# Feed-forward gate and up by seven block products, and two weight sums of every pair by adding transfers

## The chip, the cores and the metric

One core of a Trainium2 chip runs the whole program. The metric is device time in microseconds (us). The engines are TensorE (PE, matmuls), VectorE (DVE), ScalarE (ACT), GpSimd (POOL) and SyncE (SP, which issues the transfers). TensorE reads its operands from the on-chip memory SBUF and adds into the banks of PSUM.

## The reference

512 tokens (16 more, "meta", stand ahead of them) of width 1024 pass three blocks: a block of attention, a linear recurrence and a gated feed-forward part, and then two layers of a short convolution and retention. What matters here:

```python
u = rms_norm(h, norm_ffn_w[l])                      # feed-forward part; D_FF = 2816 = 22 tiles of 128
h = h + (silu(u @ w_ffn_gate[l]) * (u @ w_ffn_up[l])) @ w_ffn_down[l]
...
xn = _rmsnorm(h, pre_norm_g[l])                     # each of the two layers
proj = xn @ w_in[l] + b_in[l]
c_h, c_b, c_c, c_z, r_q, r_k, r_v, r_z, g_a, g_b = split(proj)
y_a = short_conv(c_h, c_b, c_c, c_z) @ w_out
y_b = retention(r_q, r_k, r_v, r_z) @ w_out
y = (sigmoid(g_a) * y_a + sigmoid(g_b) * y_b) @ w_o[l]
```

Everything is float32.

## The kernel before

Activations lie transposed: 128 features on the partitions, eight tiles for the width of 1024, tokens along the free axis (528, or 512 without meta). A weight tile is 128 x 1024: one output tile of 128 features, all 1024 inputs.

**Three matmuls per product.** Each float32 operand is split into a rounded high part (ACT's copy to float32r) and the rest as a low part (DVE's subtraction). `mm3` (L148 to L150) forms high x high, low x high, high x low. `unit` loads a weight tile by SP into a raw buffer `wraw` and splits it (L126 ACT, L127 DVE) into `whi` and `wlo`. There are three buffers of each of these tags.

**Seven products.** In the layers, two output tiles are formed together (`seven`): a 2 x 2 block scheme that needs seven block products where eight would do. The blocks are two output tiles, two halves of the 1024 inputs and two halves of the tokens. `pair` loads both weight tiles `sa` (a11, a12) and `sb` (a21, a22) and forms four sums of weight blocks on DVE (L201, L202, L203, L205), 128 x 512 each, which are split as well (L188 ACT, L189 DVE). The operands on the token side (n5, n6, m7, and m4 in place of a block of xs) are formed once by the generator `operands` in `layer2`, beside two plain tiles. Each product is 12 matmuls (L223); a pair is 84, of 264 columns in layer 0 and 258 in layer 1. `keep` copies a partial result out of PSUM, `sink` turns the products into outputs. `a22` and `s4` of a pair are used late, in the next pair's turn.

**Feed-forward part** (`ffn`, L869). For each of 22 tiles a gate and an up product by `mm3`: the first two tiles in two halves of the tokens (the second half waits for its normalization), the others at 512 columns. SiLU is ACT's; `fg = fg * ps` (L884) and the split into `act` are DVE's and ACT's. Then eight rows of the down projection sum over all 22 tiles, the last three rows in two halves.

**What sets the order.** Each engine runs its instructions in the order in which a scheduler laid them down when the program was built, by priority and data flow; `high_priority` moves a weight's load, splits and sums ahead. SP issues transfers in order, and each waits for its buffer to be free.

Of the kernel before, what the change touches and what calls it, by code (L numbers as in the profile page):

```python
# [59 lines left out]
class Builder:  # L60
# [52 lines left out]

    def unit(self, src, pool=None):

        nc = self.nc
        cols = src.shape[-1]
        raw = self.wp.tile([P, 1040], F32, name="wraw", tag="wraw", bufs=3)[:, :cols]
        hi, lo = (
            (pool or self.wp).tile([P, 1024 if pool else 1040], F32R, name=f"w{n}", tag=f"w{n}", bufs=KEEP if pool else 3)[:, :cols]  # L120
            for n in ("hi", "lo")
        )

        with self.tc.high_priority(offset=AHEAD):
            nc.sync.dma_start(raw, src)
            nc.scalar.activation(hi, raw, AF.Copy)  # L126
            nc.vector.tensor_tensor(lo, raw, hi.bitcast(F32), ALU.subtract)  # L127
        return hi, lo

    def loadr(self, dst, src):  # L130

        n = int(np.prod(dst.shape[1:]))
        t = self.wp.tile([P, 1040], F32, name="wraw", tag="wraw", bufs=3)[:, :n]
# [43 lines left out]
    def pair(self, sa, sb, pool):  # L177
# [6 lines left out]
        def split(names, src, where):  # L184
            n = src.shape[-1]
            hi, lo = ((self.wp if where == "w" else pool).tile(
                [P, 1040 if where == "w" else 1024], F32R, name=f"{where}{x}", tag=f"{where}{x}", bufs=3)[:, :n] for x in ("hi", "lo"))
# [5 lines left out]
        with self.tc.high_priority(offset=PAIRAHEAD):  # L193
            ra, rb = (self.wp.tile([P, 1040], F32, name="wraw", tag="wraw", bufs=3)[:, :1024] for _ in range(2))
            nc.sync.dma_start(ra, sa)
            nc.sync.dma_start(rb, sb)
            split(("a11", "a12"), ra, "w")
            s23, s14 = (pool.tile([P, 1056], F32, name="ws", tag="ws", bufs=2) for _ in range(2))
            s1, s2, s3, s4 = s14[:, :H], s23[:, :H], s23[:, H : 2 * H], s14[:, H : 2 * H]
            a11, a12, a21, a22 = ra[:, :H], ra[:, H:], rb[:, :H], rb[:, H:]  # L200
            nc.vector.tensor_tensor(s1, a21, a22, ALU.add)  # L201
            nc.vector.tensor_tensor(s2, s1, a11, ALU.add)  # L202
            nc.vector.tensor_tensor(s3, a21, a11, ALU.add)  # L203
            split(("s2", "s3"), s23[:, : 2 * H], "s")
            nc.vector.tensor_tensor(s4, s2, a12, ALU.add)  # L205
            split(("s1", "s4"), s14[:, : 2 * H], "s")
            split(("a22",), a22, "w")
        return parts

    def seven(self, units, X, n, pool):  # L210
# [29 lines left out]
        for sa, sb, sink in units:  # L240
# [628 lines left out]
    def ffn(self, h, acc, xs, last_chain):  # L869
        tc, nc, d = self.tc, self.nc, self.d  # L870
        NF = 22
        SPLIT = 3
        with tc.tile_pool(name="ff", bufs=1) as ff:
            act = tuple(ff.tile([P, NF, NX], F32R, name=f"act{s}") for s in "hl")
            gs = {}

            def gate(i, a, n, up):
                if i not in gs:
                    gs[i] = ff.tile([P, NX], F32, name="fg", tag="fg", bufs=3)
                c = slice(a - NM, a - NM + n)  # L880
                g = gs[i][:, c]
                for ps, _, _ in self.fproj(d["w_up" if up else "w_gate"][i], xs, ((a, n),)):
                    if up:
                        nc.vector.tensor_tensor(g, g, ps, ALU.mult)  # L884
                        self.split(act[0][:, i, c], act[1][:, i, c], g)
                    else:
                        nc.scalar.activation(g, ps, AF.Silu)
# [16 lines left out]
            for i, segs in parts:  # L904
                us = []
                for a, k in ((0, 8), (8, 8), (16, 6)):
                    hi, lo = self.unit(d["w_down"][i, :, a * P : (a + k) * P])
                    us.append((hi, lo, range(a, a + k), 0))
# [635 lines left out]
```

## Time and profile before

| | us |
|---|---|
| median of 3 runs | 2385.03 (2383.64 to 2392.14) |
| the profiled execution | 2390.16 |
| its span, first to last instruction | 2388.4 |
| mean granted clock of TensorE | 0.993 of full speed |
| TensorE busy | 2338.1 (98%) |
| VectorE busy | 1453.8 (61%) |
| ScalarE busy | 999.6 (42%) |
| POOL busy | 374.8 (16%) |

Busy times come from one profiled execution. A matmul's duration overlaps the next one's; the pace is read from the starts. POOL issues no transfer in this kernel.

### The profile page before, as it was taken

To read this page: it belongs to the slowest core of one execution; us is meant where nothing else is said; L and a number is where in the kernel's file an instruction comes from. 1 tells how busy PE (TensorE), PEld (TensorE's weight loads), DVE (VectorE), ACT (ScalarE), POOL (GpSimd) and SP (SyncE) were. 2 spreads that over 40 slices of the span, in tenths; PEclk is the share of its full clock that TensorE was granted. 3 is DMA by queue.
4 is the path that set the end of the run, shared out by engine and by line. 5 is a ranking of instruction groups with operands and counts; after the bars stand their busy time and mean duration, and the time that the engine had idled before them with its cause. 6 is when DMAs were issued, how large, how long until landed. Compare 5 with 4: busy or idle time off the path is not lost.

```text
span 2388.4 us, 40000 instructions
## 1 busy us (share of the span) xinstructions
PE 2338.1 (98%) x16322; PEld 2177.8 (91%) x16322; DVE 1453.8 (61%) x2560; ACT 999.6 (42%) x1751; POOL 374.8 (16%) x431
## 2 busy tenths in 40 slices
PE   8999989999999999999999999999999999999997
PEld 7888879888889999999999999999898888999987
DVE  5377786333336755555478996566455555899853
ACT  6244474222225443333335564444332423455633
POOL 3043442000003221111000020042111101000200
PEclk9999999999999999999999999999999999999999
DMA  4211203232335322222122232413222222232222
GB/s 155 87 44 59 72 19 106 97 97 90 90 100 186 119 89 84 72 83 80 63 89 98 98 105 99 131 69 111 89 84 87 77 80 78 90 107 101 97 95 71
DMA packets 67625, 217.97 MB, mean 91 GB/s; under 512 B 8816, under 2 KB 14576, under 8 KB 67440
## 3 DMA queue, kind: packets, MB, share of 16 engines
q1 hardware_dynamic: 67440, 215.40, 27.4%
q8 instruction: 128, 2.10, 0.4%
q14 instruction: 57, 0.47, 0.1%
HBM read 213.28 MB, written 2.10 MB: 90 GB/s over the span
## 4 chain that ended last, share of the span: by engine, by line
PE 87%; DVE 6%; ACT 2%; POOL 2%; issue 2%; DMA 1%; SPq 0%; DVEq 0%; ACTq 0%; POOLq 0%
PE ps L148 23%; PE ps L149 23%; PE ps L150 22%; PE ps L223 13%; PE ps L284 2%; POOL hacc L310 1%; PE ps L656 1%; PE ps L340 1%; PE ps L321 1%; DMA wraw<-in_w 1%; PE ps L1105 0%; DVE wlo L189 0%; PE ps L637 0%; ACT whi L126 0%; DVE slo L189 0%
## 5 line engine op out<-in xcount | busy, mean ns | idle before, releaser
L126 ACT ACTIVATE whi<-wraw 128x1024 fp32r<-128x1024 f32 (+1 forms) x305 | 319.3, 1050 | 690.8 <-PE ps L149 435.8
L127 DVE TENSOR_TENSOR wlo<-wraw,whi 128x1024 fp32r<-128x1024 f32 (+1 forms) x305 | 376.9, 1239 | 257.2 <-ACT whi L126 244.2
L149 PE MATMUL ps<-xsl,whi 128*128 128x264 f32 (+2 forms) x1152 | 364.5, 317 | 1.8 <-POOL xsl L143 0.9
L148 PE MATMUL ps<-xsh,whi 128*128 128x264 f32 (+2 forms) x1152 | 365.6, 317 | 0.0
L150 PE MATMUL ps<-xsh,wlo 128*128 128x264 f32 (+2 forms) x1152 | 361.5, 314 | 0.0
L148 PE MATMUL ps<-xph,whi 128*128 128x264 f32 (+4 forms) x792 | 251.4, 317 | 0.2 <-ACT xph L142 0.2
L149 PE MATMUL ps<-xpl,whi 128*128 128x264 f32 (+4 forms) x792 | 249.9, 316 | 1.4 <-DVE xpl L143 1.0
L150 PE MATMUL ps<-xph,wlo 128*128 128x264 f32 (+4 forms) x792 | 249.5, 315 | 0.0
L149 PEld LDWEIGHTS ps<-xsl,whi 128*128 128x128 f32 x1152 | 217.2, 189 | 17.7 <-POOL xsl L143 2.7
L148 PEld LDWEIGHTS ps<-xsh,whi 128*128 128x128 f32 x1152 | 217.4, 189 | 15.1 <-ACT xsh L142 0.2
L150 PEld LDWEIGHTS ps<-xsh,wlo 128*128 128x128 f32 x1152 | 217.5, 189 | 14.2
L149 PEld LDWEIGHTS ps<-xpl,whi 128*128 128x128 f32 x792 | 148.9, 188 | 12.0 <-DVE xpl L143 1.4
L148 PEld LDWEIGHTS ps<-xph,whi 128*128 128x128 f32 x792 | 149.0, 188 | 10.4 <-ACT xph L142 0.4
L150 PEld LDWEIGHTS ps<-xph,wlo 128*128 128x128 f32 x792 | 149.1, 188 | 10.2
L328 POOL TENSOR_TENSOR rs<-rs,mhalf 88x3 f32<-88x3 f32 (+4 forms) x25 | 33.2, 1330 | 780.4 <-DVE rs L326 780.4
L149 PE MATMUL ps<-srl,whi 128*128 128x264 f32 (+1 forms) x384 | 123.2, 321 | 0.0
L148 PE MATMUL ps<-srh,whi 128*128 128x264 f32 (+1 forms) x384 | 123.2, 321 | 0.0
L150 PE MATMUL ps<-srh,wlo 128*128 128x264 f32 (+1 forms) x384 | 123.1, 321 | 0.0
L189 DVE TENSOR_TENSOR slo<-ws,shi 128x1024 fp32r<-128x1024 f32 x80 | 102.9, 1296 | 10.7 <-ACT shi L188 10.3
L188 ACT ACTIVATE shi<-ws 128x1024 fp32r<-128x1024 f32 x80 | 83.9, 1057 | 35.2 <-PE ps L223 16.6
L1006 POOL TENSOR_TENSOR t<-t,t 128x264 f32<-128x264 f32 (+2 forms) x58 | 61.6, 1081 | 179.5 <-DVE t L1005 179.4
L189 DVE TENSOR_TENSOR wlo<-wraw,whi 128x1024 fp32r<-128x1024 f32 x80 | 84.9, 1061 | 7.5 <-ACT whi L188 7.2
(419 smaller groups left out, 6473.9 us busy)
## 6 DMA issues: line engine op xcount, KB each, us to landing
wraw<-in_w SPq DMA_DIRECT2D x164, 512.0 KB, 3.3
wraw<-in_wv SPq DMA_DIRECT2D x40, 512.0 KB, 3.2
wraw<-in_wr SPq DMA_DIRECT2D x32, 512.0 KB, 3.2
wraw<-in_w_gate SPq DMA_DIRECT2D x24, 512.0 KB, 3.5
wraw<-in_w_up SPq DMA_DIRECT2D x24, 512.0 KB, 3.4
wraw<-in_w_down SPq DMA_DIRECT2D x22, 512.0 KB, 3.6
wraw<-in_wc SPq DMA_DIRECT2D x16, 512.0 KB, 3.2
wraw<-in_wo SPq DMA_DIRECT2D x16, 512.0 KB, 3.3
```

The costliest lines, as they stand in the source:

```text
L126: nc.scalar.activation(hi, raw, AF.Copy)
L127: nc.vector.tensor_tensor(lo, raw, hi.bitcast(F32), ALU.subtract)
L148: nc.tensor.matmul(out, w[0], x[0], start=start, stop=False)
L149: nc.tensor.matmul(out, w[0], x[1], start=False, stop=False)
L150: nc.tensor.matmul(out, w[1], x[0], start=False, stop=stop)
L188: nc.scalar.activation(hi, src, AF.Copy)
L189: nc.vector.tensor_tensor(lo, src, hi.bitcast(F32), ALU.subtract)
L223: nc.tensor.matmul(ps, wk[p], xk[q], start=first and kt == 0 and i == 0, stop=kt == 3 and i == 2, skip_group_check=True)
L284: self.nc.tensor.matmul(ps, x2[:, kt], us[kt // 4][w][:, c : c + n], start=kt == 0 and w == 0, stop=kt == KD - 1 and w == 1,)
L310: (eng or nc.vector).tensor_tensor(dst, dst, sq, ALU.add)
L328: nc.gpsimd.tensor_tensor(r2[:m, :k], r[:m, :k], self.mhalf[:m, :k], ALU.pow)
L1006: nc.gpsimd.tensor_tensor(t1, t1, t2, op)
```

## The change

The gate and up tiles 4 to 21 of the feed-forward part become pairs of `seven`, gate and up of one tile together, at 256 columns. Since the operands of the token side take room, `act` holds 14 tiles only: tiles 0 to 7 are formed, their share of the down projection is added to h (eight rows, eight tiles each), then tiles 8 to 21 are formed and the rest of the down projection runs, its last four rows in halves. `operands` becomes a method that both places use.

In `pair`, s1 = a21 + a22 and s3 = a21 + a11 are no longer formed on DVE. SP loads a21 twice into one raw buffer (a broadcast), and two transfers issued by POOL add a22 onto the one half and a11 onto the other. DVE still forms s2 and s4. a22 is loaded by itself beside s2 and s4 in a tile `sf` (one buffer), and the three are split in one go (128 x 1536). The late product of `a22` moves ahead of that of `s3`.

```diff
@@ def pair(self, sa, sb, pool) @@
         with self.tc.high_priority(offset=PAIRAHEAD):
-            ra, rb = (self.wp.tile([P, 1040], F32, name="wraw", tag="wraw", bufs=3)[:, :1024] for _ in range(2))
+            ra, rb = (self.wtile("raw")[:, : 2 * H] for _ in range(2))
+            s13 = rb.rearrange("p (o n) -> p o n", o=2)
+            nc.sync.dma_start(s13, sb[:, :H].rearrange("p (o n) -> p o n", o=1).to_broadcast([P, 2, H]))
+            nc.gpsimd.dma_start(s13[:, 0], sb[:, H:], accum_op=ALU.add)
+            nc.gpsimd.dma_start(s13[:, 1], sa[:, :H], accum_op=ALU.add)
             nc.sync.dma_start(ra, sa)
-            nc.sync.dma_start(rb, sb)
-            split(("a11", "a12"), ra, "w")
-            s23, s14 = (pool.tile([P, 1056], F32, name="ws", tag="ws", bufs=2) for _ in range(2))
-            nc.vector.tensor_tensor(s1, a21, a22, ALU.add)
-            nc.vector.tensor_tensor(s2, s1, a11, ALU.add)
-            nc.vector.tensor_tensor(s3, a21, a11, ALU.add)
-            split(("s2", "s3"), s23[:, : 2 * H], "s")
-            nc.vector.tensor_tensor(s4, s2, a12, ALU.add)
-            split(("s1", "s4"), s14[:, : 2 * H], "s")
-            split(("a22",), a22, "w")
+            sf = pool.tile([P, 3 * H], F32, name="sf", tag="sf", bufs=1)
+            nc.sync.dma_start(sf[:, :H], sb[:, H:])
+            s2, s4 = sf[:, H : 2 * H], sf[:, 2 * H :]
+            nc.vector.tensor_tensor(s2, rb[:, :H], ra[:, :H], ALU.add)
+            nc.vector.tensor_tensor(s4, s2, ra[:, H:], ALU.add)
+            split(("a11", "a12"), ra, *(self.wtile(n)[:, : 2 * H] for n in ("hi", "lo")))
+            split(("a22", "s2", "s4"), sf, *(pool.tile([P, 3 * H], F32R, name=f"s{n}", tag=f"s{n}", bufs=2) for n in "hl"))
+            split(("s1", "s3"), rb, *(self.wtile(n)[:, : 2 * H] for n in ("hi", "lo")))
@@ def seven @@
             u = keep(a)
+            if late:
+                last(*late, 1)
             c = self.ps()[:, :n]
             prod(c, w["s3"], X["m7"], True)
-            if late:
-                last(*late, 1)
@@ def ffn @@
+        NA = 8
+        PLAIN = 4
+        SPLIT = 4
...
+            X, prep, prep4 = self.operands(xs, HALF, hn, ff)
...
+            def sink(i):
+                g, u = tile_("fg"), tile_("fu")
+                def f(j, h, ps, other):
+                    c = slice(h * hn, h * hn + hn)
+                    if j:
+                        nc.vector.tensor_tensor(u[:, c], ps, other, ALU.subtract)
+                        if h == 0:
+                            act_out(i, g, u, slice(0, NX))
+                    else:
+                        if h == 0:
+                            nc.vector.tensor_tensor(g[:, c], ps, other, ALU.add)
+                            ps = g[:, c]
+                        nc.scalar.activation(g[:, c], ps, AF.Silu)
+                return f
...
             for s in XTH:
                 if s is not XTH[0]:
                     self.finish(last_chain)
+                    prep = self.start(prep)
...
-            for i in range(2, NF):
+            for i in range(2, PLAIN):
                 for up in (False, True):
                     gate(i, *XT[0], up)
+            self.finish(prep)
+            prep4()
+            self.seven(pairs(PLAIN, NA), X, hn, ff)
+            for i in range(KD):
+                down_out(i, down(i, 0, NA), *X0[0])
+            self.seven(pairs(NA, NF), X, hn, ff)
...
-                for a, k in ((0, 8), (8, 8), (16, 6)):
-                    hi, lo = self.unit(d["w_down"][i, :, a * P : (a + k) * P])
+                us = down(i, NA, NF)
```

**How the order moves.** VectorE in layer 0's pairs, before: one pair's splits (`wlo` of a raw tile, `slo` of two sums) and the next pair's four sums (`ws`). `xpl` is the split of a convolution's product, `o1` an output of `sink`.

```order
L189 TENSOR_TENSOR wlo_13892<-wraw_13887,whi_13891 128x1024
L143 TENSOR_TENSOR xpl_12295<-y_13603,xph_12294 128x528
L189 TENSOR_TENSOR slo_13901<-ws_13895,shi_13900 128x1024
L189 TENSOR_TENSOR slo_13906<-ws_13896,shi_13905 128x1024
L189 TENSOR_TENSOR wlo_13910<-wraw_13888,whi_13909 128x512
L201 TENSOR_TENSOR ws_14026<-wraw_14018 128x512
L203 TENSOR_TENSOR ws_14025<-wraw_14018,wraw_14017 128x512
L202 TENSOR_TENSOR ws_14025<-ws_14026,wraw_14017 128x512
L1302 TENSOR_TENSOR o1_13623<-ps_13706,keep_13704 128x264
L205 TENSOR_TENSOR ws_14026<-ws_14025,wraw_14017 128x512
```

After, the same stage of the layer: L204 is s2, L205 is s4, both in `sf`.

```order
L189 TENSOR_TENSOR sl_15102<-sf_15093,sh_15101 128x1536
L204 TENSOR_TENSOR sf_15222<-wraw_15217,wraw_15216 128x512
L205 TENSOR_TENSOR sf_15222<-sf_15222,wraw_15216 128x512
L146 TENSOR_TENSOR xpl_13402<-y_14927,xph_13401 128x528
L189 TENSOR_TENSOR wlo_15227<-wraw_15216,whi_15226 128x1024
L1362 TENSOR_TENSOR o1_14960<-ps_15057,keep_15082 128x264
L1358 TENSOR_TENSOR o0_15085<-ps_15124,keep_15122 128x264
L189 TENSOR_TENSOR wlo_15235<-wraw_15217,whi_15234 128x1024
```

The four sums become two, with the split of the 1536-wide tile ahead of the next pair's s2; s2 and s4 stand ahead of the split of a11 and a12, which is the last reader of the raw tile `ra`.

SP in layer 0's pairs, before: the two weight tiles of each pair by turns.

```order
L195 DMA wraw_14150<-in_w2_0 128x1024
L196 DMA wraw_14151<-in_w2_0 128x1024
L195 DMA wraw_14280<-in_w2_0 128x1024
L196 DMA wraw_14281<-in_w2_0 128x1024
L195 DMA wraw_14413<-in_w2_0 128x1024
```

After, the same queue: L197 is the broadcast, L202 the single a22, L200 the tile `sa`.

```order
L197 DMA wraw_15472<-in_w2_0 128x2x512
L202 DMA sf_15348<-in_w2_0 128x512
L200 DMA wraw_15471<-in_w2_0 128x1024
L197 DMA wraw_15598<-in_w2_0 128x2x512
L202 DMA sf_15477<-in_w2_0 128x512
```

A pair's broadcast is now issued first, ahead of the previous pair's a22 and its own `sa`. POOL has the two adding transfers of a pair (L198, L199), in layer 0 with its product of the convolution (L1323) between them every other pair.

VectorE at the start of the feed-forward part, second half of the normalization (`nt`, `xsl`), before:

```order
L351 SCALAR_TENSOR_TENSOR nt_4432<-h_77,vec_67,ps_4408 128x264
L143 TENSOR_TENSOR xsl_3955<-nt_4424,xsh_3954 128x264
L351 SCALAR_TENSOR_TENSOR nt_4436<-h_77,vec_67,ps_4408 128x264
L351 SCALAR_TENSOR_TENSOR nt_4440<-h_77,vec_67,ps_4408 128x264
L143 TENSOR_TENSOR xsl_3955<-nt_4436,xsh_3954 128x264
L884 TENSOR_TENSOR fg_4375<-fg_4375,ps_4450 128x248
L127 TENSOR_TENSOR wlo_4546<-wraw_4544,whi_4545 128x1024
L143 TENSOR_TENSOR actl_4296<-fg_4375,acth_4295 128x248
L127 TENSOR_TENSOR wlo_4578<-wraw_4576,whi_4577 128x1024
```

After, the rows up to the weight split of the same unit (`wlo_4571`; before, `wlo_4546`):

```order
L146 TENSOR_TENSOR n5l_4298<-st_4488,n5h_4297 128x256
L242 TENSOR_TENSOR st_4488<-st_4488 128x256
L227 TENSOR_TENSOR st_4601<-xsh_3954,xsl_3955 128x256
L244 TENSOR_TENSOR st_4488<-st_4488 128x256
L146 TENSOR_TENSOR m7l_4302<-st_4488,m7h_4301 128x256
L227 TENSOR_TENSOR st_4488<-xsh_3954,xsl_3955 128x256
L146 TENSOR_TENSOR n6l_4300<-st_4488,n6h_4299 128x256
L247 TENSOR_TENSOR keep_4303<-st_4488 128x256
L238 TENSOR_TENSOR st_4601<-st_4601 128x256
L932 TENSOR_TENSOR fg_4385<-fg_4385,ps_4460 128x248
L227 TENSOR_TENSOR st_4601<-xsh_3954,xsl_3955 128x256
L130 TENSOR_TENSOR wlo_4571<-wraw_4569,whi_4570 128x1024
```

The operand chain (`st`, `n5l`, `m7l`, `n6l`; `keep` here holds the sum for m4) has moved in between the normalization and that split: 15 of its instructions stand there, ten of them in these rows.

## Rows read from the trace of the kernel before

**Rows 1.** The profile's page: busy time of the engines, and the start of the chain.

```profile
PE 2338.1 (98%) x16322; PEld 2177.8 (91%) x16322; DVE 1453.8 (61%) x2560; ACT 999.6 (42%) x1751; POOL 374.8 (16%) x431
...
PE 87%; DVE 6%; ACT 2%; POOL 2%; issue 2%; DMA 1%; SPq 0%; DVEq 0%; ACTq 0%; POOLq 0%
```

**Rows 2.** Windows by stage: stretch, length, busy time (count) per engine, granted clock, DMA.

```profile
450.00:500.00 50.00, 50.00 (x218) 40.55 (x217) 16.87 (x18) 14.15 (x19) 0.00 (x0) 1.00 0.29 95
1290.00:1440.00 150.00, 149.13 (x1220) 148.72 (x1219) 141.33 (x204) 90.17 (x142) 19.34 (x12) 1.00 0.31 103
2085.00:2138.00 53.00, 53.00 (x445) 53.00 (x444) 50.62 (x75) 31.86 (x51) 2.58 (x2) 1.00 0.34 117
2138.00:2240.00 102.00, 101.79 (x839) 100.61 (x837) 96.05 (x134) 59.68 (x96) 13.76 (x9) 1.00 0.31 102
```

**Rows 3.** Timeline of PE, feed-forward, 512 columns: start us, duration us, engine, line, operation.

```profile
430.50 0.39 PE L149 MATMUL ps<-xsl,whi 128*128 128x512 f32 x1
...
454.11 0.40 PE L149 MATMUL ps<-xsl,whi 128*128 128x512 f32 x1
```

**Rows 4.** Timeline of PE, layer 0's pairs, 264 columns.

```profile
1300.11 0.28 PE L223 MATMUL ps<-xsh,whi 128*128 128x264 f32 x1
...
1310.36 0.29 PE L223 MATMUL ps<-xsh,whi 128*128 128x264 f32 x1
```

**Rows 5.** Timeline of PE, layer 1's pairs, 258 columns.

```profile
2202.44 0.28 PE L223 MATMUL ps<-xph,whi 128*128 128x258 f32 x1
...
2212.49 0.28 PE L223 MATMUL ps<-xph,whi 128*128 128x258 f32 x1
```

**Rows 6.** Timeline of VectorE, layer 1's pairs.

```profile
2150.15 1.54 DVE L189 TENSOR_TENSOR wlo<-wraw,whi 128x1024 fp32r<-128x1024 f32 x1 [0.47 <-ACT whi L188]
...
2157.92 0.42 DVE L1302 TENSOR_TENSOR o<-ps,keep 128x258 f32<-128x258 f32 x1
2158.25 0.68 DVE L205 TENSOR_TENSOR ws<-ws,wraw 128x512 f32<-128x512 f32 x1
...
2170.61 1.53 DVE L189 TENSOR_TENSOR wlo<-wraw,whi 128x1024 fp32r<-128x1024 f32 x1 [0.47 <-ACT whi L188]
```

**Rows 7.** Lines by form, VectorE: busy us, mean ns of one, idle before.

```profile
L189 DVE TENSOR_TENSOR slo<-ws,shi 128x1024 fp32r<-128x1024 f32 x80 | 102.9, 1296 | 10.7 <-ACT shi L188 10.3 <-PE ps L223 0.3
...
L201 DVE TENSOR_TENSOR ws<-wraw 128x512 f32<-128x512 f32 x40 | 30.7, 768 | 12.7 <-DMA wraw<-in_w 12.7
...
L202 DVE TENSOR_TENSOR ws<-ws,wraw 128x512 f32<-128x512 f32 x40 | 27.4, 684 | 0.1
L205 DVE TENSOR_TENSOR ws<-ws,wraw 128x512 f32<-128x512 f32 x40 | 27.3, 682 | 0.0
...
L1256 DVE SCALAR_TENSOR_TENSOR y<-u,vec,y 128x528 f32<-128x528 f32 x16 | 12.2, 763 | 0.1
```

**Rows 8.** Timeline of VectorE, the feed-forward part's start, second half normalized.

```profile
393.30 1.29 DVE L351 SCALAR_TENSOR_TENSOR nt<-h,vec,ps 128x264 f32<-128x264 f32 x3 [1.91 <-PE ps L340]
...
394.85 1.78 DVE L127 TENSOR_TENSOR wlo<-wraw,whi 128x1024 fp32r<-128x1024 f32 x1
...
401.13 1.22 DVE L127 TENSOR_TENSOR wlo<-wraw,whi 128x1024 fp32r<-128x1024 f32 x1 [0.59 <-ACT whi L126]
...
404.55 0.43 DVE L884 TENSOR_TENSOR fg<-fg,ps 128x264 f32<-128x264 f32 x1 [0.72 <-PE ps L150]
...
410.39 0.43 DVE L884 TENSOR_TENSOR fg<-fg,ps 128x264 f32<-128x264 f32 x1 [0.74 <-PE ps L150]
```

**Rows 9.** DMA issues by line: queue, count, KB each, median us from issue to landing.

```profile
wraw<-in_w SPq DMA_DIRECT2D x164, 512.0 KB, 3.3
...
h<-in_h SPq DMA_DIRECT2D x8, 264.0 KB, 2.7
...
mask<-in_mask SPq DMA_DIRECT2D x1, 288.0 KB, 7.1
...
wraw<-in_Mk SPq DMA_DIRECT2D x1, 64.0 KB, 1.7
```

More of the change, by code (lines that the diff above doesn't have):

```diff
@@ L112, in v, with wtile @@
         return self.vec[:, a + i : a + i + 1]
+    def wtile(self, name):
+        return self.wp.tile([P, 1040], F32 if name == "raw" else F32R, name=f"w{name}", tag=f"w{name}", bufs=3)
     def unit(self, src, pool=None):
@@ L117, in unit @@
         cols = src.shape[-1]
[L118 to L122, printed above, removed]
+        raw = self.wtile("raw")[:, :cols]
+        if pool:
+            hi, lo = (pool.tile([P, 1024], F32R, name=f"w{n}", tag=f"w{n}", bufs=KEEP)[:, :cols] for n in ("hi", "lo"))
+        else:
+            hi, lo = (self.wtile(n)[:, :cols] for n in ("hi", "lo"))
         with self.tc.high_priority(offset=AHEAD):
@@ L132, in loadr @@
         n = int(np.prod(dst.shape[1:]))
-        t = self.wp.tile([P, 1040], F32, name="wraw", tag="wraw", bufs=3)[:, :n]
+        t = self.wtile("raw")[:, :n]
         if len(dst.shape) == 3:
@@ L182, in pair, with split @@
         parts = {}
[L184 to L187, printed above, removed]
+        def split(names, src, hi, lo):
             nc.scalar.activation(hi, src, AF.Copy)
@@ new lines, in pairs, with down, down_out @@
+            def pairs(i0, i1):
+                for i in range(i0, i1):
+                    yield d["w_gate"][i], d["w_up"][i], sink(i)
+            def down(i, i0, i1):
+                us = []
+                for a in range(i0, i1, KD):
+                    k = min(KD, i1 - a)
+                    hi, lo = self.unit(d["w_down"][i, :, a * P : (a + k) * P])
+                    us.append((hi, lo, range(a - i0, a - i0 + k), 0))
+                return us
+            def down_out(i, us, a, n):
+                ps = self.proj(us, act, a, n)
+                hv = h[:, i, NM + a : NM + a + n]
+                nc.vector.tensor_tensor(hv, ps, hv, ALU.add)
+                return hv
@@ L904, in ffn @@
             for i, segs in parts:
[L905 to L908 removed]
+                us = down(i, NA, NF)
                 for a, n in segs:
[L910 to L912 removed]
+                    hv = down_out(i, us, a, n)
                     sq = self.sqacc(acc, hv, NM + a, n, i == 0, last=i == KD - 1)
@@ L1215, in layer2 @@
         with tc.tile_pool(name=f"cv{l}", bufs=1) as cv:
[L1216 to L1248 removed]
+            X, prep, prep4 = self.operands(xs, HALF, hn, cv)
             tile_ = lambda tag, bufs=2, extra=0: cv.tile([P, NT + extra], F32, name=tag, tag=tag, bufs=bufs)
@@ L1263, in conv_out @@
                 self.split(ych[:, i, q0:], ycl[:, i, q0:], y[:, q0:])
-            prep = self.start(operands())
+            prep = self.start(prep)
             for i in range(PLAIN):
@@ L1286, in layer2 @@
             self.finish(prep)
-            for kt in range(4):
-                self.split(X["m4"][0][:, kt], X["m4"][1][:, kt], x4[:, kt])
+            prep4()
             def sink(bias, func, done):
```

93 lines of the change are left out of this document (50 added, 43 removed).

## The prediction

> **What bounds the kernel now.** I read the page first: the busy line and the chain of waits [rows 1]. The reader is to see that TensorE is busy 98% of the span and carries 87% of the chain, so a saving is one in matmul time, and a new wait counts where TensorE has to stand for it. Next the windows by stage [rows 2], for what the two kinds of work look like beside TensorE. In the feed-forward gate and up, VectorE is busy 16.87 of 50 us. In the layers' pairs it is busy 141.33 of 150 us (layer 0) and 96.05 of 102 us (layer 1): the pairs are where VectorE nearly is the bound.
>
> The pace of one matmul comes from its starts, not its duration, since matmuls overlap. 512 columns [rows 3]: 102 starts in 454.11 - 430.50 = 23.61 us, 0.2315 us each. One pair of the layers is 7 x 4 x 3 = 84 matmuls: 10.25 us at 264 columns [rows 4], 10.05 us at 258 [rows 5]. That is 0.033 us per pair and column, so 9.98 us at 256. The stage's windows hold 1220 matmuls in 150 us and 839 in 102 us [rows 2]; at those paces they need 148.9 and 100.4, so 1.1 and 1.6 us of TensorE are lost there. In layer 1 the loss has a period: the same weight split of VectorE starts at 2150.15 and 2170.61, 20.46 us for two pairs whose matmuls take 20.10 [rows 6].
>
> **Part 1, gate and up by seven products.** A gate tile and its up tile are now 2 x 8 x 3 = 48 matmuls of 512 columns, 48 x 0.2315 = 11.11 us. By seven products they are 84 of 256, 9.98 us. Saved 1.13 us for each of 18 tiles (4 to 21): 20.3 us, all on TensorE's path, since TensorE is without gaps there [rows 2, 3]. The down projection in two parts has the same 8 x 22 x 3 matmuls over the whole; its halved rows are 4 x 14 where they were 3 x 22, nothing to speak of. Eight more additions of its sums to h (taken like a sum of 512 columns, 0.68 us each on VectorE [rows 7]) lie beside about 5.6 us of matmuls each: nothing.
>
> **Part 2, the operands.** The chain that builds the sums of xs now also runs at the start of the feed-forward part: 44 VectorE instructions of 256 columns and four late splits. One of 258 columns holds VectorE 0.33 us from start to start [rows 6]. They stand between the normalization of the second half and the weight splits that the next gates wait for. The third unit of the second half is split at 401.13 to 402.35 now [rows 8], and TensorE comes to it when the up product of tile 0 ends, about 404.5 (the multiplication there waits for TensorE). In the new order 15 operand instructions stand ahead of that split: 15 x 0.33 = 5.0 us, about 1.2 of it in VectorE's gaps, so it ends near 406.2, 1.7 us late; later units bring some 1.3 us more until the whole 512-column tiles let VectorE catch up. I take +3 us, between 0 (the scheduler's gaps are larger) and +6 (each unit late by its full share). If the cover by the two plain tiles were gone, the first pair would wait for the rest of the chain, that +6.
>
> **Part 3, sums by transfers.** Of every pair's four weight sums two leave VectorE: 2 x 0.68 us less [rows 7], and four splits become three of the same elements. VectorE, 96.05 of 102 us and so 9.5 us of a pair of layer 1 [rows 2], falls to 8.1. That should give back most of the 1.1 + 1.6 us: I take -2 us.
>
> Against it stands a longer ring. There are three raw buffers, so the broadcast of pair k+1's second half starts only when the first half of pair k is released. The steps, by the new order, in the feed-forward part: sum s2 0.68, split of a11 and a12 1.22, sum s4 0.68 [rows 7, 8]; broadcast of 512 KB from issue to landing 3.3 [rows 9]; POOL's accumulate until it has landed, X; then s2 again. That is 5.9 + X per pair against TensorE's 9.98, so it binds above X = 4.1. In the layers the order puts other work inside: per two pairs 0.68 + 0.68 + 0.7 (the split of a conv product, taken like a sum) + 1.22 and 0.68 + 0.76 + 0.68 + 1.22, twice 3.3, twice X: 13.3 + 2X against 20.5 (layer 0) and 20.1 (layer 1), so above 3.6 and 3.4. What a pair lacks adds up over a run, but a run starts with the next pair's sums ready, about one pair's time less the VectorE steps: 10 - 3 = 7 us of stock. Runs: 4 and 14 pairs in the feed-forward part (the first without stock), 18 in each layer.
>
> X stands in no row: no accumulating transfer and no transfer from POOL is in this trace. From below, a plain transfer of about its size, 264 KB: 2.7; from above the slowest of that size, 288 KB in the crowd at the start: 7.1 [rows 9]. The accumulate has to read the tile as well as the weights, so by bytes read it is the row of 512 KB, 3.3. Behind the broadcast 256 KB and 512 KB of plain loads are issued on the same engines, so I add one step of those rows, 3.3 - 2.7 = 0.6: X = 3.9. Then the feed-forward ring is 9.8 (hidden), layer 0 lacks 0.6 x 9 = 5.4 (within the 7 of stock), layer 1 lacks 1.0 x 9 - 7 = 2 us. I take +2.
>
> The Trainium skill, Collectives: The Full Stack, section Why ReduceScatter is half of AllGather, says that an add inside the transfer engines costs not for the add but for its second source read. No run here shows it yet. By that rule the transfer counts as 512 KB, as I counted it; without it X would be 3.3 and the +2 would be 0.
>
> POOL is idle in most of these stretches [rows 2], but its queue is in order: in layer 0 the second accumulate of every other pair stands behind POOL's conv product. It feeds s3 alone, which TensorE needs late in the pair, so I cost it at nothing.
>
> **Sum**, against the profiled execution's own time of 2390.2: -20.3 + 3 - 2 + 2 = -17.3, so 2372.9. The median of the runs shown is 5.1 us lower, 2385.0; the forecast for a median is 2385.0 - 17.3 = 2368 us.
>
> **Rivals.**
> A (forecast): X at most 4.1. Its own range is 2361 (no operand stall, all 2.7 us given back, no ring loss: -20.3 - 2.7 = -23) to 2374.
> B, the gain is eaten: X about 4.5. The feed-forward ring's 0.4 x 14 stays in stock, its first run without stock costs 0.4 x 4 = 2; layer 0 lacks 1.8 x 9 - 7 = 9, layer 1 2.2 x 9 - 7 = 13. -20.3 + 3 - 2 + 24 = +5: 2390. For it: X must beat the next higher step by little. Against: transfers here land close to their medians.
> C, slower: the ring is the bound, from X of about 4.9 on. The place is s2 on VectorE waiting for the accumulate, in every pair. At X = 5: feed-forward 0.9 x 14 - 7 + 0.9 x 4 = 9, layers 2.8 x 9 - 7 = 18 and 3.2 x 9 - 7 = 22; -19.3 + 49 = +30: 2415. At 5.5 it is +58. For it: POOL's share of the issue is unknown, and transfers of this size have taken 7.1 [rows 9]. Against: that row is of a crowd, and a pair's transfers here are 512 + 512 + 256 + 2 x 256 KB in 10 us.
> D, a form of C: POOL can't write its descriptors while VectorE holds a port. If each accumulate waits for one of VectorE's long splits, 1.3 us [rows 7], X is 3.9 + 1.3 = 5.2: feed-forward 13, layers 22 and 25, so -19.3 + 60 = +41, 2426. VectorE is busy over 94% of those stages now [rows 2], which speaks for it. The Trainium skill, SBUF — State Buffer, section SBUF: two separate sides, has this trap for a VectorE operation in a two-port mode; no run here shows it, and nearly all of VectorE's work here has two inputs, which that section's table keeps out of the trap.
> That the seven products don't save is hardly possible: two layers show their pace.
>
> **How the numbers follow.** A 0.50, B 0.26, C 0.18, D 0.06. About 0.5% (12 us) is what a measurement tells from no change. A lies under 2373 nearly whole, faster 0.48; B and A's rest are within, 0.28; C and D slower, 0.24. Range: 2361, the best that the sum allows, to 2415, C at X = 5; what is left out is C's far end and D, under 0.15, and little below.
>
> **What would show it.** Right: 18 tiles with starts of 256 columns 0.119 us apart; a gap of TensorE of about 3 us before the first pair and hardly any in the pairs; VectorE's s2 waiting for a transfer, but with TensorE's idle in the layers' runs at 2 to 3 us; accumulates landing in under 4.1 us. Wrong: TensorE's gaps recurring once per pair behind a weight split that waits for s2, with accumulates above 4.5; or VectorE above 95% in the feed-forward pairs, which would make its in-order queue the bound instead; or a stall of over 6 us at the feed-forward part's start.

## The result and the profile after

| | before | after |
|---|---|---|
| median, run side by side (us) | 2387.64 (2383.64 to 2392.14) | 2441.61 (2440.33 to 2444.63) |
| span of the profiled execution | 2388.4 | 2438.5 |
| mean granted clock | 0.993 | 0.986 |

The change made the kernel slower: ratio 1.0227, 95% interval 1.0211 to 1.0243, some 54 us. The forecast was 2368, with a range that ended at 2415.

The page of after, the lines that answer to [rows 1]:

```profile
PE 2338.7 (96%) x16940; PEld 2208.7 (91%) x16940; DVE 1505.1 (62%) x2605; ACT 1048.1 (43%) x1817; POOL 472.0 (19%) x547
...
PE 76%; DVE 8%; DMA 7%; ACT 3%; POOL 3%; issue 3%; SPq 0%; ACTq 0%; DVEq 0%; POOLq 0%
```

TensorE's share of the chain fell from 87% to 76%, and transfers rose from 1% to 7%. What TensorE waited for, by the view of waits (us in total, times, longest), first of after, then the same wait in before:

```profile
PE ps L269 <- ACT keep L275: 47.0, 21, 7.1
PE ps L886 <- POOL pt L876: 7.4, 7, 2.0
PE ps L151 <- ACT xh L479: 7.1, 1, 7.1
```

```profile
PE ps L223 <- ACT keep L229: 0.9, 1, 0.9
```

So nearly all of the new idle time is one wait: a product of `seven` waits for ScalarE's copy out of PSUM (`keep`). The copy itself is short; what has to be found is what stands ahead of it in ScalarE's queue.

Windows of after (stretch, length, busy time and count of PE, PEld, DVE, ACT, POOL, granted clock, DMA share, GB/s): the first pairs of the feed-forward part, the middle of its second run, and two of the stretches of [rows 2].

```profile
436.00:480.00 44.00, 37.85 (x294) 37.49 (x294) 29.97 (x41) 22.28 (x35) 3.55 (x4) 0.88 0.58 150
550.00:650.00 100.00, 99.62 (x840) 99.38 (x839) 77.84 (x102) 58.24 (x90) 17.91 (x20) 1.00 0.74 188
1290.00:1440.00 150.00, 142.07 (x1142) 139.53 (x1141) 116.89 (x149) 82.72 (x119) 38.80 (x39) 1.00 0.68 167
2138.00:2240.00 102.00, 96.64 (x769) 94.98 (x768) 81.76 (x100) 53.52 (x77) 20.92 (x22) 0.97 0.66 164
```

In the middle of the feed-forward run 840 matmuls start in 100 us, 0.119 us each: ten pairs at TensorE's full pace, transfers and all. In the layers the same 150 and 102 us hold 78 and 70 matmuls fewer than before. And at the first pairs of the feed-forward part the granted clock averages 0.88: it fell during a wait of 7.1 us that ended at 442.15, and it was at the lower of its two levels (1.2 of 2.4 GHz) from 438 to 446, so still for some 4 us of matmuls. Two microseconds there hold 12 matmuls, and 19 at the full clock:

```profile
438.00:446.00 8.00, 3.85 (x18) 3.85 (x19) 7.74 (x12) 4.90 (x7) 1.76 (x2) 0.50 0.47 112
444.00:446.00 2.00, 2.00 (x12) 2.00 (x11) 2.00 (x4) 1.50 (x3) 0.93 (x2) 0.50 0.93 165
450.00:452.00 2.00, 2.00 (x19) 2.00 (x18) 1.97 (x3) 1.63 (x4) 0.00 (x0) 1.00 0.78 276
```

Transfers of after, the lines that answer to [rows 9] (KB each, median us to landing):

```profile
wraw<-in_w SPq DMA_DIRECT2D x164, 512.0 KB, 4.2
...
wraw<-in_w POOLq DMA_DIRECT2D x80, 256.0 KB, 4.9
...
wraw<-in_w_up POOLq DMA_DIRECT2D x18, 256.0 KB, 4.8
wraw<-in_w_gate POOLq DMA_DIRECT2D x18, 256.0 KB, 7.4
```

The accumulates take 4.8 to 7.4 us (medians). The first line's 4.2, where before has 3.3, mixes 84 loads outside the pairs with those of the pairs; the pairs' own loads (L197 and L200) both have a median of 4.9.

Lengths of the stages (us), read from the starts of matmuls: the feed-forward part from the last product of the attention's output to the last of the down projection, the long run of 18 pairs of a layer from its first to its last product on n5, n6 or m7, and the two single pairs behind it from there to their last such product. The last seven rows are the experiments that follow.

| kernel | feed-forward | layer 0 long | single pairs | layer 1 long | single pairs |
|---|---|---|---|---|---|
| before | 380.7 | 181.4 | 45.2 | 179.1 | 42.6 |
| after | 377.5 | 195.0 | 56.0 | 194.6 | 53.9 |
| e1, sums by VectorE | 363.8 | 182.5 | 44.4 | 181.0 | 42.5 |
| e3, conv product on VectorE | 383.2 | 183.2 | 55.7 | 180.0 | 54.5 |
| e4, no accumulates | 363.8 | 186.6 | 44.4 | 184.2 | 42.8 |
| e5, plain transfers | 370.3 | 188.8 | 51.8 | 187.0 | 45.2 |
| e6, first two pairs by VectorE | 369.6 | 184.4 | 44.7 | 180.8 | 44.1 |
| e13, ties at the ends, conv on VectorE | 376.1 | 184.1 | 44.3 | 181.9 | 46.7 |
| e14, ties at the ends | 376.2 | 198.5 | 46.3 | 197.0 | 44.3 |

The losses of after add up: -3.2 + 13.6 + 10.8 + 15.5 + 11.3 = 48.0 of the 50.1 us between the spans.

Beside e1, which runs the same 16940 matmuls, after is 68.0 us longer, and not all of that is waiting. TensorE idles 47.3 us more, and the same matmuls take 20.7 us more (2338.7 us in after, and in e1

```profile
PE 2318.0 (98%) x16940; PEld 2192.8 (93%) x16940; DVE 1569.1 (66%) x2779; ACT 1062.4 (45%) x1875; POOL 374.5 (16%) x431
```

at a mean granted clock of 0.986 for 0.995). In the single pairs, where the waits are longest for their length, the clock is 0.94 and in e1 1.00.

**Where it stands, at a run's start.** Timeline of after, first pairs of the feed-forward part, all engines in order of time:

```profile
424.26 0.38 SPq L197 DMA_DIRECT2D wraw<-in_w_up  x1
428.57 0.87 POOL L198 DMA_DIRECT2D wraw<-in_w_up  x1 [10.14 <-DVE sl L189]
429.97 0.33 SPq L200 DMA_DIRECT2D wraw<-in_w_gate  x1
430.81 1.32 ACT L145 ACTIVATE xsh<-keep 128x256 fp32r<-128x256 f32 x4
434.82 0.28 PE L269 MATMUL ps<-xsh,wlo 128*128 128x256 f32 x1
436.89 0.69 DVE L204 TENSOR_TENSOR sf<-wraw 128x512 f32<-128x512 f32 x1 [6.34 <-DMA wraw<-in_w_gate]
439.40 1.48 ACT L188 ACTIVATE sh<-sf 128x1536 fp32r<-128x1536 f32 x1 [7.27 <-issue]
440.79 1.04 ACT L188 ACTIVATE whi<-wraw 128x1024 fp32r<-128x1024 f32 x1
441.74 0.36 ACT L275 ACTIVATE keep<-ps 128x256 f32<-128x256 f32 x1
442.15 0.58 PE L269 MATMUL ps<-n6h,sh 128*128 128x256 f32 x1 [7.06 <-ACT keep L275]
```

TensorE stops at 435.1 in the first pair and needs the copy of its first product. That copy runs at 441.74, because ScalarE's queue has the *second* pair's splits (439.40, 440.79) ahead of it, and these wait for that pair's broadcast (424.26), accumulate (428.57), first half (429.97) and sums (436.89 and on). Last to land is the first half, a plain load: by the trace's landings the accumulate is there at 433.50 and the first half at 436.76, 6.8 us after its issue. In 45 of the 58 pairs the first half lands after the first accumulate. The first pair itself lacks nothing.

**Where it stands, in the layers.** The same view, layer 0's long run:

```profile
1316.23 0.38 SPq L197 DMA_DIRECT2D wraw<-in_w  x1
1319.63 0.72 ACT L1388 ACTIVATE o<-o,vec 128x528 f32<-128x528 f32 x1
1321.72 0.87 POOL L198 DMA_DIRECT2D wraw<-in_w  x1 [8.32 <-DVE sl L189]
1322.29 1.66 POOL L1323 TENSOR_TENSOR y<-y,o 128x528 f32<-128x528 f32 x1
1323.98 0.64 ACT L145 ACTIVATE xph<-y 128x528 fp32r<-128x528 f32 x1 [1.74 <-POOL y L1323]
1324.53 0.65 ACT L275 ACTIVATE keep<-ps 128x264 f32<-128x264 f32 x2
1324.96 0.39 PE L269 MATMUL ps<-xsh,sh 128*128 128x264 f32 x1 [0.76 <-ACT keep L275]
```

Here the queue at fault is POOL's. The conv product's last operand is ready at 1320.35 (1319.63 + 0.72) and POOL is idle, but an accumulate stands ahead of it that waits for its broadcast (issued at 1316.23). The product starts 1.9 us late, ScalarE's split of it waits 1.74 us, the copies stand behind that split, and TensorE behind them. It recurs once in two pairs of the conv: all 14 waits for a copy in the two long runs, 21.0 us, stand behind such a split.

### The profile page after: what moved, and what is told of

It reads as the page before. It is cut to its first block, busy times and chain, and to the rows that moved or that the text cites. A ratio compares the mean times of both kernels' runs of the same rounds, so it can differ in the third digit from the quotient of the medians.

```text
span 2438.5 us, 41923 instructions
## 1 busy us (share of the span) xinstructions
PE 2338.7 (96%) x16940; PEld 2208.7 (91%) x16940; DVE 1505.1 (62%) x2605; ACT 1048.1 (43%) x1817; POOL 472.0 (19%) x547
## 3 DMA queue, kind: packets, MB, share of 16 engines
q0 software_dynamic: 16704, 30.42, 7.9%
## 4 chain that ended last, share of the span: by engine, by line
PE 76%; DVE 8%; DMA 7%; ACT 3%; POOL 3%; issue 3%; SPq 0%; ACTq 0%; DVEq 0%; POOLq 0%
PE ps L151 18%; PE ps L152 17%; PE ps L269 17%; PE ps L153 17%; DMA wraw<-in_w 4%; PE ps L330 2%; DMA wraw<-in_w_gate 1%; DVE wlo L189 1%; DVE wlo L130 1%; POOL hacc L356 1%; PE ps L702 1%; PE ps L386 1%; DMA wraw<-in_w_up 1%; POOL y L1323 1%; ACT whi L129 1%
## 5 line engine op out<-in xcount | busy, mean ns | idle before, releaser
L152 PE MATMUL ps<-xsl,whi 128*128 128x264 f32 (+2 forms) x864 | 251.1, 291 | 3.0 <-DVE xsl L146 1.7
L151 PE MATMUL ps<-xsh,whi 128*128 128x264 f32 (+2 forms) x864 | 252.2, 292 | 0.5 <-ACT whi L129 0.3
L153 PE MATMUL ps<-xsh,wlo 128*128 128x264 f32 (+2 forms) x864 | 249.0, 288 | 1.6 <-DVE wlo L130 1.6
L188 ACT ACTIVATE whi<-wraw 128x1024 fp32r<-128x1024 f32 x116 | 122.9, 1059 | 111.2 <-PE ps L269 66.5
L152 PEld LDWEIGHTS ps<-xsl,whi 128*128 128x128 f32 x864 | 163.2, 189 | 7.0 <-POOL xsl L146 2.9
L153 PEld LDWEIGHTS ps<-xsh,wlo 128*128 128x128 f32 x864 | 163.6, 189 | 3.2 <-DVE wlo L130 1.8
L151 PEld LDWEIGHTS ps<-xsh,whi 128*128 128x128 f32 x864 | 163.3, 189 | 2.9 <-ACT whi L129 0.5
L189 DVE TENSOR_TENSOR wlo<-wraw,whi 128x1024 fp32r<-128x1024 f32 x116 | 154.3, 1338 | 2.9 <-ACT whi L188 2.4
L188 ACT ACTIVATE sh<-sf 128x1536 fp32r<-128x1536 f32 x58 | 86.3, 1489 | 104.9 <-PE ps L269 46.4
L189 DVE TENSOR_TENSOR sl<-sf,sh 128x1536 fp32r<-128x1536 f32 x58 | 101.9, 1757 | 30.3 <-ACT sh L188 30.3
```

Source lines behind the costliest of these rows:

```text
L151: nc.tensor.matmul(out, w[0], x[0], start=start, stop=False)
L152: nc.tensor.matmul(out, w[0], x[1], start=False, stop=False)
L153: nc.tensor.matmul(out, w[1], x[0], start=False, stop=stop)
L188: nc.scalar.activation(hi, src, AF.Copy)
L189: nc.vector.tensor_tensor(lo, src, hi.bitcast(F32), ALU.subtract)
```

## Experiments

**e1 and e8, the feed-forward part alone.** `pair` as before, everything else as after, but for one buffer fewer of the up tile (e8 also has the late product in its old place); from the edit:

```diff
-            s13 = rb.rearrange("p (o n) -> p o n", o=2)
-            nc.sync.dma_start(s13, ...to_broadcast([P, 2, H]))
-            nc.gpsimd.dma_start(s13[:, 0], sb[:, H:], accum_op=ALU.add)
-            nc.gpsimd.dma_start(s13[:, 1], sa[:, :H], accum_op=ALU.add)
+            nc.sync.dma_start(rb, sb)
...
+            nc.vector.tensor_tensor(s1, a21, a22, ALU.add)
+            nc.vector.tensor_tensor(s3, a21, a11, ALU.add)
```

> The gate and up by seven products as in the changed kernel, but all four weight sums of a pair made by VectorE as before (no transfer adds; one buffer fewer for the up tile, to make room). Theory 1 (latency: what loses time is the chain broadcast, wait on POOL, accumulate, which has to end before a pair's sums can start, and which stands open at every start of a run of pairs): without that chain the 20 us of the seven products stay and only the operand stall of about 2 us remains, so 18 us less than before, about 2368 to 2372. Rival (the feed-forward part loses at its own starts, whatever makes the sums): the feed-forward part is only 5 us shorter, as in the changed kernel, about 2382.

> The feed-forward part alone changed, sums by VectorE, and the order of the late product as before (after the product of s3). In the first kernel of this kind the layers' long runs were 1.1 and 1.7 us longer than before. If the order did that, this one is 2 to 3 us faster, about 2371; if not, the same 2374.

Measured: e1 2374.39 us, ratio 0.9949 (0.9933 to 0.9964); e8 2375.02, 0.9944 (0.9929 to 0.9959). The feed-forward part is 17.0 us shorter than before (363.8 against 380.7), and its VectorE keeps up with all four sums. The rival is out. The old order gave 180.5 and 177.8 us for the long runs where e1 has 182.5 and 181.0, but the two times can't be told apart. TensorE's wait for the copies is down to one of 0.7 us; the longest entry of `seven` in e1 is

```profile
PE ps L271 <- DVE o L1364: 4.7, 8, 1.3
```

**e2, the new `pair` in the layers alone.** `ffn` as before, `pair` as after:

> The sums by adding transfers in the layers alone; the feed-forward part as before, gate and up by plain products. By stage the changed kernel lost 14.9 and 17.5 us in the long runs of pairs of the two layers and 11.6 and 12.1 in the short runs behind them. If these losses belong to the transfers alone, this kernel is 56 us slower than before, about 2443. If part of them comes from what the feed-forward part leaves behind (clock, tiles), it is less: 2420 to 2430.

Measured: 2437.55 us, 1.0214 (1.0198 to 1.0230), 51 us slower; the long runs take 192.7 and 189.8 us, the single pairs 55.2 and 52.5. The loss belongs to the new `pair`, its transfers and its layout, and not to what the feed-forward part leaves behind; e4 and e7 tell the two apart.

**e3, the conv product off POOL's queue:**

```diff
-                nc.gpsimd.tensor_tensor(y[:, q0:], y[:, q0:], sz[:, q0:], ALU.mult)
+                nc.vector.tensor_tensor(y[:, q0:], y[:, q0:], sz[:, q0:], ALU.mult)
```

> The changed kernel with the conv product moved from POOL to VectorE. Theory 2 (POOL's queue: the conv product stands behind an accumulate that waits for its broadcast, ScalarE's split of it and the copy out of PSUM behind that split wait too, and TensorE waits for the copy): the gaps of 0.8 to 1.3 us that recur once in two pairs of the conv go, some six in each layer, so 12 to 15 us less than the changed kernel, about 2427. Theory 1 alone: the recurring gaps stay, no change to 2441, or 2 us more from VectorE's added work.

Measured: 2420.41 us, 1.0137 (1.0115 to 1.0160): 21 us less than after, more than expected. The long runs go from 195.0 and 194.6 to 183.2 and 180.0, the single pairs stay. POOL's queue cost those runs 11.8 and 14.6 us. (The feed-forward part of e3 runs the same instructions in the same order as that of after: its 383.2 us beside 377.5 shows how far two executions of it can lie apart.) Left of the wait:

```profile
PE ps L269 <- ACT keep L275: 28.2, 9, 7.1
```

**e4, no accumulates** (the two `nc.gpsimd.dma_start` lines taken out, so that the sums lack a22 and a11):

> The changed kernel without its two accumulating transfers per pair; the broadcast stays. It leaves out the adding of a22 and a11 into the two sums, so VectorE's load is that of the changed kernel and POOL issues nothing. Theory 1 (latency of the chain): the stalls at the starts of runs shrink by the accumulate's 4.5 to 7 us and nearly vanish, so 2365 to 2375. Theory 3 (bytes: the broadcast and the second load of a22 slow all loads beside them): a part of the loss stays, 2400 or more, and the loads of 512 KB still land in 4 to 5 us.

Measured: 2382.35 us, 0.9982 (0.9972 to 0.9993). Feed-forward part and single pairs are as in e1, to 0.3 us. The broadcast and the second load of a22 are still there, and so is the new layout, so it is the accumulates that cost the time and not these bytes: theory 3 is out. The loads of a pair's first half land in 3.2 us again. The broadcast doesn't quite: 4.2 us, where after has 4.9 (e4, first the broadcast, then the first half):

```profile
DMA to landing us min/median/max: 3.5/4.2/5.6
...
DMA to landing us min/median/max: 3.1/3.2/4.9
```

In e7, below, the first of a pair's three loads is a plain one and has a median of 4.0, so this part belongs to the new row of loads more than to the broadcast.

**e5, the same transfers without the add** (`accum_op` taken out, so that the sums lack a21):

> The changed kernel with its two accumulating transfers per pair as plain transfers from POOL: same bytes written, same waits for the broadcast, no reading of the tile and no addition (it leaves out the adding of a21 into the two sums). If the add itself (reading the tile) is what makes the accumulate slow, these land in about 2.7 to 3 us, like 256 KB loads of SyncE, loads of 512 KB beside them go back to about 3.5, and the stalls at the starts shrink by 2 us each: about 2420 to 2425. If it is POOL's way of issuing or the crowd, they still land in 4.5 us or more and the time stays within 5 us of 2441.

Measured: 2408.79 us, 1.0085 (1.0070 to 1.0100), better than either branch: 33 us less than after. The 26 us that e5 still has over e4 come with the two transfers as such, add or no add. POOL's transfers land in 3.7 us (page of e5) where they took 4.9, and POOL holds its queue 0.54 us for one where the add takes 0.87 (the form's minimum, median and maximum in ns; below, the landings of all first transfers of a pair, and for after of the second ones too; first e5, then after):

```profile
wraw<-in_w POOLq DMA_DIRECT2D x80, 256.0 KB, 3.7
...
q0 software_dynamic: 9280, 30.42, 3.8%
...
L198 POOL DMA_DIRECT2D wraw<-in_w x40: 536/538/626, 1238.0 to 2288.8; - x40
...
DMA to landing us min/median/max: 3.0/3.5/5.4
```

```profile
q0 software_dynamic: 16704, 30.42, 7.9%
...
L198 POOL DMA_DIRECT2D wraw<-in_w x40: 852/867/932, 1243.9 to 2319.8; - x40
...
DMA to landing us min/median/max: 3.6/4.5/7.4
...
DMA to landing us min/median/max: 4.0/6.6/8.6
```

The queue's line says what the add costs: the same 30.42 MB, in 16704 packets for 9280, take twice the engines' time. The Trainium skill, Collectives: The Full Stack, section Why ReduceScatter is half of AllGather, puts the cost of a collective's add down to its second source read; 7.9% against 3.8% fits that, though the line doesn't show what the added packets read.

**e6, the starts of runs by VectorE.** On e3: in the first two pairs of every run, so in all single pairs, a21 and a22 are loaded plainly and s1 and s3 are formed in place:

```diff
+            if lead:
+                nc.sync.dma_start(ra, sa)
+                nc.sync.dma_start(rb, sb)
...
+                nc.vector.tensor_tensor(s1, rb[:, :H], s1, ALU.add)
...
+                nc.vector.tensor_tensor(rb[:, :H], rb[:, :H], ra[:, :H], ALU.add)
```

> The kernel with the conv product on VectorE, and besides the first two pairs of every run (so the short runs whole) with their sums by VectorE in place; the other pairs by transfers. Theory 1 (the transfers cost at the starts of runs and in the short runs, where the chain stands open, and nearly nothing in the middle of a run): the 11 to 12 us of each layer's short runs come back and most of the starts, so 2375 to 2385. Rival (the ring of three raw buffers costs in whichever pairs come first by transfers): the short runs come back, 23 us, but the starts move two pairs on and cost as before: about 2395 to 2400.

Measured: 2387.43 us, 0.9992 (0.9982 to 1.0001): some 34 us less than e3, near theory 1. The single pairs are back at 44.7 and 44.1. The last two pairs of a layer's long run are a call of their own and count as a run, so 42 of the 58 pairs still use the transfers. They lose little: TensorE's wait for the copies is 8.8 us in all, and the feed-forward part has 5.8 us over e1.

**e7, all sums by VectorE in the new layout** (e6's form for every pair, conv product on POOL):

> The changed kernel's layout, order of products and three splits, its conv product on POOL, but all sums of all pairs by VectorE in place and no transfer that adds. Both theories: the time of the kernel with the feed-forward part alone changed, 2372 to 2376. If the new layout (one buffer for a22 and two sums, a split of 1536) or the order of the last products costs something of its own, it is above 2380, with gaps in the layers' long runs.

Measured: 2403.05 us, 1.0064 (1.0048 to 1.0081): the layout with its sums by VectorE costs something of its own, some 28 us against e1. The feed-forward part takes 369.6 us, the long runs 193.1 and 191.9, and two waits share it:

```profile
PE ps L279 <- ACT keep L285: 14.3, 19, 2.7
PE ps L279 <- DVE o L1372: 10.0, 12, 1.8
```

Which of its parts does it (the one buffer for a22, s2 and s4, their long split, or sums in place) was not separated. The layout alone is not enough: e4 has it, without the two sums, and takes 363.8, 186.6 and 184.2 us there.

**e9, e10 and e12, a tie in every pair.** A ScalarE instruction of one column reads the second copy and the tile `sf`, so that the next pair's long split must come behind the copies (e10 with the conv product on VectorE, e12 on e6):

```diff
             u = keep(a)
+            tie = pool.tile([P, 2], F32, name="tie", tag="tie", bufs=2)[:, :1]
+            nc.scalar.activation(tie, u[:, :1], AF.Identity, bias=w["sf"][:, :1])
```

> The changed kernel with one more ScalarE instruction per pair, of one column, that reads the pair's second copy out of PSUM and its tile of sums: by it the tile is free for the next pair only after that copy, so the next pair's split of 1536 stands behind the copies in ScalarE's queue, where it stood ahead of them at the starts of runs. Theory 1a (it is the order of that queue that turns the late sums into a wait of TensorE): the gap of 7.1 us at the first pair and those of 4 to 5 us in the short runs fall under 2 us, so 15 to 25 us less than the changed kernel, 2417 to 2427. Rival 1b (the sums are late whatever the order): the gaps move to the next pair's first product, 2436 to 2446, or more for the longer chain.

> The same with the conv product on VectorE. If the two causes are separate, the savings add: 21 us of the conv product and what the run before this shows, 2396 to 2406 by theory 1a. By 1b no better than the conv product alone, 2420.

> The kernel whose first two pairs of each run have their sums by VectorE, conv product on VectorE, with the tie as well. By theory 1a its gaps of 2.7 and 1.0 us in the feed-forward part and 1.2 to 1.8 us in the layers go: about 2380, between 2375 and 2385; no better than the 2374 of the sums by VectorE alone, since what the transfers relieve, VectorE, is not what TensorE waits for. By 1b unchanged, 2387.

Measured: e9 2455.46 (1.0276, 1.0259 to 1.0293), e10 2454.76 (1.0266, 1.0241 to 1.0290), e12 2425.63 (1.0163, 1.0136 to 1.0189): all slower than the kernels that they start from. At the first pair the gap did fall from 7.06 to 3.43 us, but now `sf`, which has one buffer, comes free late in many pairs: sums of e9 waited (us, times)

```profile
  ACT tie L300: 23.7, 25
```

for the tie, and its feed-forward part takes 394.6 us. The edit lengthened the middle of the runs, so it didn't tell 1a from 1b.

**e11, buffers of its own for the second half** (feed-forward part, runs of 6 and 12 pairs):

```diff
+            rb = pool.tile([P, 2 * H], F32, name="rb", tag="rb", bufs=2) if "ff" in pool.name else ...
...
-        NA = 8
+        NA = 10
```

> The changed kernel with two buffers of its own for a pair's second half in the feed-forward part, beside the three raw ones (its runs are 6 and 12 pairs, to make room). The ring of the prediction (the broadcast waits for the first half of the pair before) can't bind there then. If the ring costs the feed-forward part its gain, the first three pairs of a run fall from 11 to 14 us apart to about 10, and the stalls of 7.1 and 2.1 us go, so 10 to 14 us less than the changed kernel, 2427 to 2432. If it is the first chain's latency with ScalarE's order, at most 4 us less.

Measured: 2443.63 us, 1.0219 (1.0195 to 1.0243), the same as after; feed-forward part 379.0 us. Gaps of 5.47 and 2.61 us stand one pair later. Three raw buffers are not what costs the gain; but two buffers of its own are a ring too, so a start without any ring wasn't tried.

**e13 and e14, ties at the ends of runs only.** The same tie, at the first pair of a long run (on its second copy) and at the last pair of every run (on its last copy):

```diff
+            if k == 0 and count > 2:
+                tie(u, w)
...
+            if k == count - 1:
+                tie(v, w)
```

> The kernel with the conv product on VectorE, and the tie only at the first pair of a run and at the last one, so that the middle of the runs is as without it and only there the next pair's split of 1536 stands behind the copies. Theory 1a (the queue's order): the gaps of 7.1, 2.1 and 4 to 5 us shrink to 1 or 2 us each, the middle stays at TensorE's pace, so 2420 - 20 = about 2400. Rival 1b (late whatever the order): the gaps reappear at the next pair's first products, 2415 to 2425.

> The changed kernel with the same ties at the first and last pairs alone, the conv product on POOL. By 1a about 20 us less than the changed kernel, 2420; by 1b 2436 to 2446.

Measured: e13 2393.60 us, 1.0026 (1.0007 to 1.0046), 27 less than e3; e14 2424.99, 1.0163 (1.0146 to 1.0180), 17 less than after. ScalarE's queue at the first pair, timeline of e13:

```profile
434.05 1.32 ACT L145 ACTIVATE xsh<-keep 128x256 fp32r<-128x256 f32 x4
439.78 1.06 ACT L188 ACTIVATE whi<-wraw 128x1024 fp32r<-128x1024 f32 x1 [4.40 <-DMA wraw<-in_w_gate]
440.74 0.61 ACT L145 ACTIVATE acth<-fg 128x512 fp32r<-128x512 f32 x1
441.26 0.36 ACT L276 ACTIVATE keep<-ps 128x256 f32<-128x256 f32 x1
```

The long split no longer stands ahead of the copy, but another split does (439.78), which waits for the pair's first half; the gap is 2.80 us. The single pairs are nearly whole again: e14 has 46.3 and 44.3 us, after 56.0 and 53.9, e1 44.4 and 42.5, so the queue's order was 9.7 of 11.6 us and 9.6 of 11.4, theory 1a. (The long runs of e14 pay 3.5 and 2.4 us for the ties.) In the feed-forward part the ties bring 1.3 us in e14; the 7.1 that e13 has less than e3 can't be credited to them, since after and e3 lie 5.7 apart with the same instructions there. Some 12 us against e1 stay: the first pairs still wait several times for a copy or a split. That speaks for 1b there, the lateness itself. With both queues mended the wait for copies is down from 47.0 to

```profile
PE ps L270 <- ACT keep L276: 11.9, 9, 2.8
```

The version that beats both kernels is the simplest: e1, seven products in the feed-forward part and no adding transfers, 2374.39 us.

## Why the prediction was wrong

**Part 1 and part 2: right.** 20.3 us of matmul time less 3 of operand stall, -17.3; e1 has -17.0 in that part, where TensorE's busy time falls by 20.0 (377.55 to 357.51). In after the stall for a split at the operands' place is one gap of 1.56 us at 402.62, within the 0 to 6 but half of the 3.

**Part 3, the relief: smaller than forecast, and of no use.** Over layer 1's long run of 18 pairs VectorE's busy time fell from 163.5 to 147.6 us, 0.9 a pair where I had 1.4. (The 81.76 of 102 us above are of a window with 70 matmuls fewer.) It had only 1.1 and 1.6 us to give back, and e3's long runs are no shorter than before.

**Part 3, X: mis-sized.** I took 3.9 us for an accumulate, by bytes read; the first of a pair lands in 4.5 us (median of its line), the second in 6.6. I left the broadcast at the 3.3 us of [rows 9]; its line has 4.9, of which 0.7 us comes with the accumulates (e4 has 4.2) and the rest without them. And the load of the first half, which the sum of the steps doesn't have at all, went from 3.2 (e4) to 4.9 and is mostly what lands last.

**Part 3, the ring and its stock: the step that failed.** The forecast added +2 us for all that the transfers cost; beside e1 after takes 68 us more, some 59 of them with the accumulates (the medians of after and e4). That "a run starts with the next pair's sums ready" is not so. The second pair's sums start 14.5 us after the first's (L204 at 422.40 and 436.89), the next 13.0 and 10.6 behind. And the list of runs, "4 and 14 pairs in the feed-forward part (the first without stock), 18 in each layer", left out the two single pairs behind each layer's long run, which are nothing but starts: 22 of the 50 us between the spans. The ring itself, from which the times of B and C were worked out, does not bind in the middle of a run. With the measured steps, 4.9 for the broadcast and 4.5 for X, it would need 12.0 us a pair; in the feed-forward part pairs follow each other in 9.9 us. There the broadcast is issued some 15 us ahead of its sum (633.05 for the sum at 648.63), and 5.7 us ahead of the sum of the pair just before (638.75): it does not wait for that pair's first half. Why the buffers come free in that order was not looked into. So C's "At 5.5 it is +58" meets the measured time by luck and is not the explanation: its place, VectorE's s2 in every pair, is not where TensorE waits. (By its own sum that is +57, and the forecast's lower end 2362 where it says 2361; nothing hangs on either.)

**POOL's queue: costed at nothing, 21 us by the medians of e3 (26 by its two long runs).** I saw that an accumulate stands behind the conv product and asked who waits for the accumulate. The costly direction is the other: the conv product stands behind an accumulate that waits for its broadcast, and ScalarE, its copies and TensorE stand behind the product (e3).

**ScalarE's queue: not asked about at all.** I named VectorE's s2 as the waiting instruction and looked at what follows it on VectorE. Behind s2 and s4 comes ScalarE's split, and behind that in its queue the copies of the pair that TensorE is in the middle of (e13 and e14: 27 and 17 us).

**TensorE's clock: not asked about either, 20.7 us.** The sum took every matmul at the pace of rows with a granted clock of 1.00 [rows 2]. With the waits the clock fell too, as at 438 to 446, and beside e1 the same matmuls took that much longer.

**Rival D: no sign.** POOL holds its queue 852 to 932 ns for every first accumulate of the layers, whatever VectorE does, and all 58 of them start 0.6 to 1.0 us after their broadcast has landed. The Trainium skill, SBUF — State Buffer, section SBUF: two separate sides, keeps tensor operations with two inputs, which VectorE's mostly are here, out of its trap for POOL's transfers; that agrees.

**What stays open:** why the feed-forward part costs some 12 us against e1 even with the ties. The layout alone is not the reason, since e4 has it and takes 363.8 us as e1 does. Of the 12.5 us 7.8 are idle time and 4.7 are slower matmuls (that part in e1, then in e14):

```profile
375.43:739.18 363.75, 357.51 (x2541) 333.66 (x2540) 265.95 (x408) 180.67 (x292) 22.46 (x22) 1.00 0.34 111
376.36:752.60 376.24, 362.21 (x2540) 337.01 (x2539) 242.85 (x354) 175.91 (x278) 54.79 (x58) 0.99 0.53 145
```

That the late sums make the idle time is argued, not shown.

## What to carry to other kernels

A transfer that replaces an engine's instruction takes that work off a busy engine and puts a latency of two transfers in series in its place; count it at every start of a run, and count the short runs. Then, for each instruction that will now wait, list what stands behind it in its own engine's queue *and* in the queues of those that consume it: here a wait of some microseconds on POOL and on ScalarE became TensorE's through instructions that had nothing to do with the transfer. And before relieving an engine, look whether the bound engine waits for it at all: here it did for 2.7 us.

## What was not expected of the hardware

An accumulating transfer costs on three sides: its own landing (256 KB in 4.5 to 6.6 us, 3.5 to 3.8 without the add), its issue on POOL (0.87 and 1.22 us for the two of a pair, 0.54 without), and the loads beside it (the 512 KB of a pair's first half in 4.9 us, 3.2 without). And while POOL multiplied 528 columns (1322.29 to 1323.95), VectorE's addition of 512 columns beside it took 2.23 us, where one takes 0.69 (timeline of after); beside nine of the sixteen such products a VectorE instruction took 1.5 to 1.9 us longer than it does alone:

```profile
1321.55 0.69 DVE L204 TENSOR_TENSOR sf<-wraw 128x512 f32<-128x512 f32 x1
1322.28 2.23 DVE L205 TENSOR_TENSOR sf<-sf,wraw 128x512 f32<-128x512 f32 x1
```
